# Nine instead of six feed-forward pairs as seven block products in the first layer, with other PSUM banks for the down products

## The chip, the cores and the metric

The kernel runs on one core of one Trainium2 chip. The metric is the device time of one execution in microseconds (us). A core has a matrix engine (TensorE, PE in the profile), a vector engine (VectorE, DVE), a scalar engine (ScalarE, ACT), GpSimd (POOL) and a sync engine (SyncE, SP) that only issues transfers. Matrix products go to PSUM, eight banks of 512 float32 columns on 128 partitions, and are copied out of it by ACT or DVE. Each engine works through its own queue in order. An instruction that waits holds up all that stands behind it on the same engine.

## The reference

Two layers of a decoder trunk over 528 tokens (16 learned ones and 512 real ones) of width 1024. Each layer is a mixer (attention, a convolution module, a short convolution, an output projection) and a feed-forward part (FFN). The change touches the FFN:

```python
def ffn_sublayer(h, pre_g, post_g, w_up, conv_w, w_down):
    u = rms_norm(h, pre_g)
    z = jnp.einsum("bld,df->blf", u, w_up)          # 1024 -> 2 x 2816
    z = causal_depthwise_conv(z, conv_w)            # 3 taps
    g, up = jnp.split(z, 2, axis=-1)
    y = jnp.einsum("blf,fd->bld", jax.nn.silu(g) * up, w_down)   # 2816 -> 1024
    return h + rms_norm(y, post_g)
```

All data are float32.

## The kernel before, in words

Activations lie transposed: 128 channels on the partitions, the 528 tokens along the free dimension. Every float32 operand is split in two float32r numbers, high and low, and a product is made of three matmuls (high x high, low x high, high x low). A weight block of 128 output columns is loaded as one tile `raw` (512 KB) by SP, ACT casts it to `whi`, DVE subtracts to get `wlo`. `next_w` (and `prefetch`, `prep_one` beneath it) keeps three blocks ready; `whi` and `wlo` have three buffers, so a cast waits until TensorE has finished the block three before. `raw_tile` gives out three `raw` buffers and, within the FFN, four more in the tile `h`, which lies in DRAM (`h_dram`) meanwhile.

**The FFN.** The 2816 hidden channels are 22 pairs f = 0 to 21, a gate block and an up block of 128 columns each. They come in three parts of 8, 7 and 7 pairs (`PARTS`): f = 0 to 7, 8 to 14, 15 to 21. After each part come the eight down products m = 0 to 7 of that part. The result of a down product is copied (part 0, ACT, L2403) or added (part 1, DVE, L2405) to `yp`.

**An ordinary pair** takes for each of two blocks 8 row groups x 3 matmuls x 2 token halves, 96 matmuls of 264 columns in the first layer, into the bank pairs 6-7 and 2-3.

**A pair as seven products** (`seven_pair`, L2285) splits the 1024 rows in two halves and the tokens in two halves, and forms the 2 x 2 blocks with seven block products instead of eight, of 12 matmuls each: 84 matmuls of 264 columns (258 in the second layer). It uses three banks, 0 to 2 and 3 to 5 in turn. It needs sums of token blocks (`ts`, made once in each layer by `normalised`), and sums of weight blocks, which lie in DRAM as `w_sum`. Of the up block it then loads three parts in place of one: "c" and "b" of 512 KB from `w_sum` and "d" of 256 KB from the weights. "c" is split to `whi`, `wlo`; "b" to `shi`, `slo`, of which there is one buffer; "d" to the spare tile `y7`. The order of use in a pair is: gate block, c, b, gate, c, b, d. The first layer has six such pairs (15 to 20), the second twelve (8 to 13 and 15 to 20): `SEVEN`.

**Where the weight sums are made.** (1) In the mixer, by a planner that places all of the mixer's work by costs (`sum_steps` through `flow.op`, lowest priority): copies DRAM to DRAM by SP, then three accumulating DMAs by POOL (L533). (2) In the FFN by `tick` (L2196): at each pair one of the four steps of a sum, behind a small POOL copy that waits for the newest gate result. (3) During the down products of parts 0 and 1, two each, by `down_sums`: loads by POOL into `h`, four DVE additions, stores by POOL (L602). In the first layer, the sums of 15 and 16 come from its own mixer, and its `tick` makes those of f = 8 and 9 of the second layer at f = 1 to 8.

**Splits made ahead.** Six blocks of the second layer's input projection are split during part 1 of the first layer and stored in DRAM as `w_split`: `store_one` (L657) is called once at each pair f = 8 to 14. Each call splits the block fetched by the call before (ACT L662 to `shi`, DVE L663 to `slo`), stores both by POOL (L666), and fetches the next block by SP (L671).

**Order.** In the FFN the order of each engine's instructions comes from a list scheduler, which works on program order and modelled times; the engines hold to it at run time. `tc.issue_after(x)` fixes that what is traced in it stands behind x on x's own engine; it is an order, not a wait for another engine. In the mixer and in the last down products the planner sets the order.

The four lines that choose the banks and the place of the splits (before):

```python
tiles = [mmt((6, 2)[m % 2]) if seven else mmt() for m in some]   # L2386
if l == 0 and part == 1:                                          # L2342
    store_one()
todo = deque(step for to, place in ((l, 2), (l + 1, 0)) ...)      # L2194
```

Of the kernel before, what the change touches and what calls it, by code (L numbers as in the profile page):

```python
# [10 lines left out]
F32 = mybir.dt.float32  # L11
# [11 lines left out]
DEPTH = 2  # L23
# [5 lines left out]
PARTS = (8, 7, 7)  # L29


SEVEN = ((15, 16, 17, 18, 19, 20), (8, 9, 10, 11, 12, 13, 15, 16, 17, 18, 19, 20))
SUMS = {0: (0, 2, 0), 1: (2, 4, 2)}
DOWN_SUMS = 2
SUM_US, SUM_LAT, SUM_EVERY = 0.9, 9.0, 40.0
K2 = KD // 2
SB = K2 * P
# [336 lines left out]
def stt_us(n):  # L374
    return 0.22 + 0.00102 * n
# [13 lines left out]
def tile_hybrid_trunk(ctx: ExitStack, tc: tile.TileContext, xT, wflat, pv_d, out):  # L389
    nc = tc.nc  # L390
# [156 lines left out]

    def sums_at(l, place):

        counts = SUMS.get(l, ())  # L550
        n0 = sum(counts[:place])
        return SEVEN[l][n0:n0 + counts[place]] if place < len(counts) else ()

    pw_place = [None]

# [5 lines left out]
            return pw_place[0][:, :n] if tag == "whi" else pw_place[0][:, n:2 * n]  # L561
        return T(wx[0], [P, WCHUNK], F32R, tag) if i in wide else T(wp, [P, CHUNK], F32R, tag)

    parts, last_load, last_low = deque(), [None], [None]
    spare, n_raw = [None], [0]

    def spare_tile(j):
# [39 lines left out]

    def down_sums(l, part):

        fs = SEVEN[l][-2 * DOWN_SUMS:][DOWN_SUMS * part:DOWN_SUMS * (part + 1)]  # L610
        at = {}
        for j, f in enumerate(fs):
            load, add, store = down_sum(l, f, j % 2)
            for m, op in ((2 * j - 1, load), (2 * j + 1, add), (2 * j + 1 + (j < 2), store)):
                at.setdefault(m, []).append(op)
        return at

    def prep_one():
        i = wpos[0]
        if i >= len(chunks):  # L620
            return
        if i in seven_up:
            if not parts:
                t = sums[seven_up[i]]
                parts.extend((("c", t[:, 1::2]), ("b", t[:, 0:3:2]), ("d", flat_w(i)[:, SB:])))
            kind, src = parts.popleft()
            wpos[0] += not parts
            raw = raw_tile()
            sz = SB if kind == "d" else 2 * SB
            nc.sync.dma_start(raw[:, :sz] if kind == "d" else raw[:, :sz].rearrange("p (e s) -> p e s", e=2),  # L630
                              src)
            if kind == "b":
                hi, lo = (T(tx[0], [P, 2 * SB], F32R, t) for t in ("shi", "slo"))
            elif kind == "c":
                hi, lo = (T(wp, [P, CHUNK], F32R, t) for t in ("whi", "wlo"))
            else:
                hi, lo = y_pair(max(PARTS) - 1)
            nc.scalar.copy(hi[:, :sz], raw[:, :sz])
            last_low[0] = nc.vector.tensor_sub(lo[:, :sz], raw[:, :sz], hi[:, :sz].bitcast(F32))
            ready.append((i, tuple(t[:, :sz].rearrange("p (k n) -> p k n", n=P) for t in (hi, lo))))  # L640
            return
        wpos[0] += 1
        kn, n = chunks[i][3], chunk_cols(chunks[i])
        sz = kn * n
        raw = raw_tile()
        last_load[0] = nc.sync.dma_start(raw[:, :sz], wflat[offs[i]:offs[i] + P * sz].rearrange("(p s) -> p s", p=P))
        hi, lo = wtile(i, "whi"), wtile(i, "wlo")
        nc.scalar.copy(hi[:, :sz], raw[:, :sz])  # L648
        last_low[0] = nc.vector.tensor_sub(lo[:, :sz], raw[:, :sz], hi[:, :sz].bitcast(F32))  # L649
        ready.append((i, tuple(t[:, :sz].rearrange("p (k n) -> p k n", n=n) for t in (hi, lo))))  # L650
# [1374 lines left out]
    with tc.tile_pool(name="pre", bufs=2, reuse_waits="tile") as sp, tc.manual_schedule(engines=every):  # L2025
# [64 lines left out]
    for l in range(DEPTH):  # L2090
# [23 lines left out]
        with tc.tile_pool(name=f"fp{l}", bufs=2, reuse_waits="tile") as fp:  # L2114
# [76 lines left out]
            h7 = [(i0, i0 + n7), (L - n7, L)]  # L2191
            late_ups = deque()
            seven = SEVEN[l]
            todo = deque(step for to, place in ((l, 2), (l + 1, 0)) for f in sums_at(to, place) for step in sum_steps(to, f))  # L2194

            def tick(src):  # L2196

                if todo:
                    t = nc.gpsimd.tensor_copy(ticks, src.bitcast(F32))
                    with tc.issue_after(t.ins):  # L2200
                        todo.popleft()()
# [62 lines left out]
            building = [None]  # L2264
# [71 lines left out]
            g = {}  # L2336
            f0 = 0
            for part, nf in enumerate(PARTS):
                for f in range(f0, f0 + nf):
                    if g:  # L2340
                        tick(g[max(g)][0][:, :1])
                    if l == 0 and part == 1:  # L2342
                        store_one()
                    if f in seven:
                        seven_pair(f)
                        if f == seven[-1]:
                            spare[0] = None
                            with tc.issue_after(last_load[0].ins):
                                for k in range(0, KD, 2):
                                    nc.sync.dma_start(h[:, k:k + 2], h_dram[:, k:k + 2])  # L2350
                        continue
                    finish_pair()
                    if seven and f == 2:
                        building[0] = normalised()
                    for i in (2 * f, 2 * f + 1):
                        if i < len(zs):
                            continue
                        if i < FIRST["w_out"]:
                            scaled(i, [first.ps[hf, i] for hf in range(2)])
                            continue  # L2360
                        w = next_w()
                        ps = mmt((6, 2)[i % 2]) if ts else mmt()
                        mm3({hf: ps[:, hf, :iws[hf]] for hf in range(2)}, w, range(KD), u_in)
                        if ts:
                            for (a, z), hf in zip(i_spans, range(2)):
                                nc.scalar.copy(zs[i % len(zs)][:, off + a - i0:off + z - i0], ps[:, hf, :z - a])
                            continue
                        scaled(i, [ps[:, :, :H]] if i0 == 0 else [ps[:, hf, :iws[hf]] for hf in range(2)])
                    g[f] = ffn_gate(f)
                    if building[0] is not None and f < PARTS[0] - 1:  # L2370
                        with tc.issue_after(mul_ins[0].ins):
                            build(5)
# [7 lines left out]
                if part < len(PARTS) - 1:  # L2380
# [2 lines left out]
                        op()  # L2383
                    for some in ((0, 1), *((m,) for m in range(2, KD))):
                        ws = [next_w() for _ in some]
                        tiles = [mmt((6, 2)[m % 2]) if seven else mmt() for m in some]  # L2386
                        for group in (ks[:-1], ks[-1:]):
                            for w, ps in zip(ws, tiles):
                                where = {"start": group[0] == ks[0], "stop": group[-1] == ks[-1]}
                                if final:  # L2390
                                    mm3({0: ps[:, 0, :2 * fw]}, w, group, lambda b, k, hf, f0=f0: g[f0 + k][b][:, :2 * fw], **where)
                                else:
                                    mm3({hf: ps[:, hf, :fw] for hf in range(2)}, w, group, grhs, **where)
                        if building[0] is not None:
                            with tc.issue_after(glo_ins[0].ins):
                                build(99)
                        for m, ps in zip(some, tiles):
                            if final:
                                d, src = yp[:, m, t0:], ps[:, 0, :2 * fw]
                            else:  # L2400
                                d, src = two(yp[:, m, t0:]), ps[:, :, :fw]
                            if part == 0:
                                evac = glo_ins[0] = nc.scalar.copy(d, src)  # L2403
                            else:
                                evac = nc.vector.tensor_add(d, d, src)  # L2405
                            for op in more.pop(m, ()):
                                with tc.issue_after(evac.ins), tc.issue_after(last_low[0].ins):
                                    op()
                else:
                    assert not todo and building[0] is None  # L2410
# [6 lines left out]
                    if not final:  # L2417
                        raw = list(zip(*[g[f0 + k] for k in range(nf)], y_pair(nf)))
# [65 lines left out]
```

## Time and profile before

| | us |
|---|---|
| median of three runs | 1269.38 (1269.15 to 1270.08) |
| the profiled execution | 1270.68 |
| its span, first to last instruction | 1269.0 |
| PE busy | 1249.8 |
| DVE busy | 920.9 |
| ACT busy | 705.2 |
| POOL busy | 162.0 |

In the trace, the first layer's FFN takes its first down products from about 353.5 us, its part 1 pairs run from 401.0 to 483.1, the down products of part 1 to 524.2, and part 2 follows. The second layer's seven-product pairs of part 1 begin at 1030.5. A line of the profile names the line of the kernel, the engine, the operation, and output<-inputs. `h<-in_w_dram` is a weight load into the lent tile. The bracket in a timeline line gives the idle time of the engine just before, and what ended it.

### The profile page before, as it was taken

To read this page: it belongs to the slowest core of one execution; us is meant where nothing else is said; L and a number is where in the kernel's file an instruction comes from. 1 tells how busy PE (TensorE), PEld (TensorE's weight loads), DVE (VectorE), ACT (ScalarE), POOL (GpSimd) and SP (SyncE) were. 2 spreads that over 40 slices of the span, in tenths; PEclk is the share of its full clock that TensorE was granted. 3 is DMA by queue.
4 is the path that set the end of the run, shared out by engine and by line. 5 is a ranking of instruction groups with operands and counts; after the bars stand their busy time and mean duration, and the time that the engine had idled before them with its cause. 6 is when DMAs were issued, how large, how long until landed. Compare 5 with 4: busy or idle time off the path is not lost.

```text
span 1269.0 us, 24272 instructions
## 1 busy us (share of the span) xinstructions
PE 1249.8 (98%) x9590; PEld 1198.2 (94%) x9590; DVE 920.9 (73%) x1569; ACT 705.2 (56%) x1365; POOL 162.0 (13%) x343
## 2 busy tenths in 40 slices
PE   8999999999999999999999999999999999999997
PEld 8998898999999999999999988999999799979996
DVE  7887866589874665587688878656799748756954
ACT  7254576654444643476673545775554447526763
POOL 1324311001101100000003244110021000000000
PEclk9999999999999999999999999999999999999999
DMA  7257231726558634544552584547166655475611
GB/s 243 81 155 175 72 102 53 249 86 151 182 164 313 212 112 142 205 165 144 192 205 61 159 191 113 143 118 233 70 166 184 172 176 169 152 241 160 202 61 67
DMA packets 76146, 197.93 MB, mean 156 GB/s; under 512 B 8240, under 2 KB 18608, under 8 KB 75520
## 3 DMA queue, kind: packets, MB, share of 16 engines
q1 hardware_dynamic: 64048, 162.69, 40.0%
q0 software_dynamic: 11984, 33.69, 11.1%
q8 instruction: 75, 1.23, 0.4%
q14 instruction: 39, 0.32, 0.1%
HBM read 162.17 MB, written 44.30 MB: 163 GB/s over the span
## 4 chain that ended last, share of the span: by engine, by line
PE 66%; DVE 2%; ACT 1%; issue 0%; DMA 0%; POOL 0%; DVEq 0%; ACTq 0%
PE psum L833 45%; PE psum L2281 14%; PE psum L1403 2%; PE psum L1667 2%; PE psum L970 1%; PE psum L1633 1%; PE psum L1589 0%; DMA h<-w_sum 0%; DVE yp L1046 0%; PE psum L1733 0%; PE psum L1319 0%; DVE h L1056 0%; POOL dm L1604 0%; DVE ulo L1064 0%; DVE wlo L649 0%
## 5 line engine op out<-in xcount | busy, mean ns | idle before, releaser
L833 PE MATMUL psum<-y,whi 128*128 128x264 f32 (+3 forms) x1968 | 384.7, 299 | 2.7 <-ACT yp L2403 1.4
L833 PEld LDWEIGHTS psum<-y,whi 128*128 128x128 f32 x1968 | 305.1, 188 | 17.2 <-ACT yp L2403 2.6
L833 PE MATMUL psum<-uhi,whi 128*128 128x264 f32 (+1 forms) x1264 | 310.3, 288 | 1.6 <-ACT uhi L2065 0.8
L833 PE MATMUL psum<-ulo,whi 128*128 128x264 f32 (+1 forms) x1264 | 304.1, 284 | 0.6 <-DVE ulo L2067 0.4
L833 PE MATMUL psum<-uhi,wlo 128*128 128x264 f32 (+1 forms) x1264 | 303.2, 284 | 0.0
L833 PE MATMUL psum<-y,wlo 128*128 128x264 f32 (+3 forms) x984 | 273.9, 297 | 1.1 <-DVE wlo L789 1.1
L833 PEld LDWEIGHTS psum<-uhi,whi 128*128 128x128 f32 x1264 | 216.0, 188 | 5.9 <-issue 1.6
L833 PEld LDWEIGHTS psum<-ulo,whi 128*128 128x128 f32 x1264 | 216.1, 188 | 1.3 <-DVE ulo L2067 0.6
L833 PEld LDWEIGHTS psum<-uhi,wlo 128*128 128x128 f32 x1264 | 215.6, 188 | 0.0
L833 PEld LDWEIGHTS psum<-y,wlo 128*128 128x128 f32 x984 | 177.6, 188 | 6.7 <-DVE wlo L789 1.6
L2169 DVE SCALAR_TENSOR_TENSOR c<-zs,pv,c 128x528 f32<-128x528 f32 (+1 forms) x176 | 130.9, 757 | 18.4 <-ACT c L2167 16.4
L648 ACT CAST whi<-raw 128x1024 fp32r<-128x1024 f32 (+1 forms) x67 | 68.2, 1021 | 98.4 <-PE psum L833 72.6
L789 DVE TENSOR_TENSOR wlo<-raw,whi 128x1024 fp32r<-128x1024 f32 (+2 forms) x80 | 95.4, 1203 | 29.8 <-ACT whi L785 29.5
L649 DVE TENSOR_TENSOR wlo<-raw,whi 128x1024 fp32r<-128x1024 f32 (+1 forms) x67 | 79.4, 1185 | 28.1 <-ACT whi L648 28.0
L785 ACT CAST whi<-raw 128x1024 fp32r<-128x1024 f32 (+2 forms) x80 | 81.7, 1031 | 24.9 <-PE psum L833 18.0
L1149 DVE SCALAR_TENSOR_TENSOR cacc<-apad,pv,cacc 128x528 f32<-128x528 f32 x120 | 87.7, 772 | 0.1
L2167 ACT ACTIVATE c<-zs,pv 128x528 f32<-128x528 f32 (+1 forms) x88 | 63.1, 727 | 7.0 <-DVE zs L2132 2.7
L2281 PE MATMUL psum<-uhi,whi 128*128 128x258 f32 (+1 forms) x216 | 61.2, 284 | 0.0
L2281 PE MATMUL psum<-ulo,whi 128*128 128x258 f32 (+1 forms) x216 | 61.0, 283 | 0.0
L2281 PE MATMUL psum<-uhi,wlo 128*128 128x258 f32 (+1 forms) x216 | 60.5, 282 | 0.0
L2281 PE MATMUL psum<-t,shi 128*128 128x258 f32 (+1 forms) x288 | 54.2, 283 | 0.0
L1667 PE MATMUL psum<-pf,vals 128*128 128x400 f32 (+3 forms) x160 | 50.7, 399 | 0.6 <-POOL pf L1647 0.6
(273 smaller groups left out, 2193.2 us busy)
## 6 DMA issues: line engine op xcount, KB each, us to landing
raw<-in_w_dram SPq DMA_DIRECT2D x115, 512.0 KB, 4.5
h<-in_w_dram SPq DMA_DIRECT2D x27, 512.0 KB, 4.8
raw<-in_w_dram SPq DMA_DIRECT2D x30, 448.0 KB, 5.1
raw<-w_sum SPq DMA_DIRECT2D x18, 512.0 KB, 5.1
h<-w_sum SPq DMA_DIRECT2D x18, 512.0 KB, 5.4
h<-in_w_dram POOLq DMA_DIRECT2D x16, 512.0 KB, 3.8
w_sum<-h POOLq DMA_DIRECT2D x16, 512.0 KB, 5.3
w_sum<-in_w_dram SPq DMA_DIRECT2D x20, 256.0 KB, 5.0
```

Of the source, the lines that this page charges most:

```text
L648: nc.scalar.copy(hi[:, :sz], raw[:, :sz])
L649: last_low[0] = nc.vector.tensor_sub(lo[:, :sz], raw[:, :sz], hi[:, :sz].bitcast(F32))
L785: nc.scalar.copy(box["hi"][:, :sz], box["raw"][:, :sz])
L789: nc.vector.tensor_sub(lo[:, :sz], box["raw"][:, :sz], box["hi"][:, :sz].bitcast(F32))
L833: nc.tensor.matmul(d, lhsT=w[a][:, k, cols], rhs=rhs(b, k, hf), start=start and i == 0 and p == 0, stop=stop and i == n - 1 and p == 2)
L970: nc.tensor.matmul(ps, lhsT=om_d, rhs=box["c"][:, i, :], start=j + i == 0, stop=j + 1 == n_parts and i == tiles[-1])
L1149: nc.vector.scalar_tensor_tensor(conv[j], in0=src, in1=conv[j], scalar=col("a_dw_w", CK * j + i), op0=ALU.mult, op1=ALU.add)
L1403: nc.tensor.matmul(ps[:n, :nw], lhsT=(uhi, ulo)[ui][:, k, P * b:P * b + n], rhs=w[wi][:, k % 4, :], start=k == 0 and p == 0, stop=k == KD ...
L1667: nc.tensor.matmul(acc[:, s0 - qa:qz - qa], lhsT=vals[:, b].rearrange("p h d -> p (h d)")[:, o:o + P], rhs=box["p"], start=b == 0, stop=b ...
L2167: nc.scalar.activation(dst, src[:, 2:2 + 2 * fw], AF.Copy, scale=wtap(2, t))
L2169: nc.vector.scalar_tensor_tensor(dst, in0=src[:, i:i + 2 * fw], scalar=wtap(i, t), in1=dst, op0=ALU.mult, op1=ALU.add)
L2281: nc.tensor.matmul(psum[:, bank, :n7], lhsT=w[a][:, k0 + k, :], rhs=rhs(b, k), start=start and k == 0 and p == 0, stop=stop and k == K2 - ...
```

## The change

`SEVEN` of the first layer grows from six pairs to nine: f = 11, 12 and 13 are added. The table `SUMS` now names the pairs for each place: in the first layer, 11 to 13 in the mixer (three sums where two were), 15 and 16 by `tick` at f = 1 to 8, 17 to 20 in the down products as before. The second layer's 8 and 9 move to the ticks from f = 14 on (`NEXT_SUMS`). The second layer's own table is as it was. `store_one` is called at f = 8, 8, 9, 9, 10, 10, 11 instead of once at each of 8 to 14. In both layers the down products of parts 0 and 1 use three bank pairs, 4-5, 6-7 and 2-3, in turn. In both layers, the load, the cast and the subtraction of a block b stand behind those of the block prepared just before it among b, c and d, which is its c.

```diff
-SEVEN = ((15, 16, 17, 18, 19, 20), (8, 9, 10, 11, 12, 13, 15, 16, 17, 18, 19, 20))
-SUMS = {0: (0, 2, 0), 1: (2, 4, 2)}
-DOWN_SUMS = 2
+SUMS = (((), (11, 12, 13), (15, 16), (17, 18), (19, 20)),
+        ((8, 9), (10, 11, 12, 13), (15, 16), (17, 18), (19, 20)))
+SEVEN = tuple(sorted(sum(places, ())) for places in SUMS)
+NEXT_SUMS, AHEAD_SPLITS = 13, (8, 8, 9, 9, 10, 10, 11)
...
     def sums_at(l, place):
-        counts = SUMS.get(l, ())
-        n0 = sum(counts[:place])
-        return SEVEN[l][n0:n0 + counts[place]] if place < len(counts) else ()
+        return SUMS[l][place] if l < DEPTH else ()
...
     def down_sums(l, part):
-        fs = SEVEN[l][-2 * DOWN_SUMS:][DOWN_SUMS * part:DOWN_SUMS * (part + 1)]
-        for j, f in enumerate(fs):
+        for j, f in enumerate(sums_at(l, 3 + part)):
...
-            nc.sync.dma_start(raw[:, :sz] if kind == "d" else raw[:, :sz].rearrange("p (e s) -> p e s", e=2),
-                              src)
+            with ExitStack() as order:
+                for x in last if kind == "b" else ():
+                    order.enter_context(tc.issue_after(x.ins))
+                load = nc.sync.dma_start(raw[:, :sz] if kind == "d" else raw[:, :sz].rearrange("p (e s) -> p e s", e=2), src)
...
-            nc.scalar.copy(hi[:, :sz], raw[:, :sz])
-            last_low[0] = nc.vector.tensor_sub(lo[:, :sz], raw[:, :sz], hi[:, :sz].bitcast(F32))
+            with ExitStack() as order:
+                for x in last if kind == "b" else ():
+                    order.enter_context(tc.issue_after(x.ins))
+                high = nc.scalar.copy(hi[:, :sz], raw[:, :sz])
+                last_low[0] = nc.vector.tensor_sub(lo[:, :sz], raw[:, :sz], hi[:, :sz].bitcast(F32))
+            last[:] = load, high, last_low[0]
...
-            todo = deque(step for to, place in ((l, 2), (l + 1, 0)) for f in sums_at(to, place) for step in sum_steps(to, f))
+            todo, later = (deque(step for f in sums_at(to, place) for step in sum_steps(to, f)) for to, place in ((l, 2), (l + 1, 0)))
             def tick(src):
+                if max(g) + 1 >= NEXT_SUMS:
+                    todo.extend(later)
+                    later.clear()
...
-                    if l == 0 and part == 1:
+                    for _ in range(AHEAD_SPLITS.count(f) if l == 0 else 0):
                         store_one()
...
-                        tiles = [mmt((6, 2)[m % 2]) if seven else mmt() for m in some]
+                        tiles = [mmt((4, 6, 2)[m % 3]) if seven else mmt() for m in some]
```

More of the change, by code (lines that the diff above doesn't have):

```diff
@@ L562, in wtile @@
         return T(wx[0], [P, WCHUNK], F32R, tag) if i in wide else T(wp, [P, CHUNK], F32R, tag)
-    parts, last_load, last_low = deque(), [None], [None]
+    parts, last_load, last_low, last = deque(), [None], [None], []
     spare, n_raw = [None], [0]
@@ L2409, in tile_hybrid_trunk @@
                 else:
-                    assert not todo and building[0] is None
+                    assert not todo and not later and building[0] is None
                     if seven:
```

## The prediction

> **What bounds the kernel now.** I read the page first, then who waited for whom on TensorE, then the busy time by stretches, then the timeline at each place where TensorE stood.
>
> ```profile
> span 1269.0 us, 24272 instructions
> PE 1249.8 (98%) x9590; PEld 1198.2 (94%) x9590; DVE 920.9 (73%) x1569; ACT 705.2 (56%) x1365; POOL 162.0 (13%) x343
> PEclk9999999999999999999999999999999999999999
> PE 66%; DVE 2%; ACT 1%; issue 0%; DMA 0%; POOL 0%; DVEq 0%; ACTq 0%
> PE psum L833 <- ACT yp L2403: 1.4, 2, 1.0
> PE psum L833 <- DVE yp L2405: 0.3, 1, 0.3
> ```
>
> TensorE is busy for 1249.8 of 1269.0 us, with a granted clock of nine tenths or more in every slice. The other engines matter only where they make it stand. So the change is worth the matmuls that it removes, plus the stalls that it removes, less those that it brings. Two of its waits name the copies of down products (L2403, L2405).
>
> **Seven instead of eight block products.** Three pairs lose 12 of 96 matmuls each, 36 together. Matmul rows overlap, so their own length (about 284 ns) is no price. The stretch that holds exactly the seven ordinary pairs of part 1 gives the interval:
>
> ```profile
> 401.00:483.10 82.10, 82.10 (x675) 82.10 (x674) 49.33 (x56) 43.90 (x72) 6.40 (x12) 1.00 0.50 167
> 1030.50:1090.00 59.50, 59.50 (x496) 59.34 (x495) 46.34 (x61) 43.44 (x78) 1.42 (x3) 1.00 0.53 167
> ```
>
> 82.10 us over 7 x 96 = 672 matmuls (the 675 count neighbours cut by the edges) are 0.122 us each, so a pair takes 11.7 us and 36 matmuls are **4.4 us**. The second row is the same arrangement as the new one, the second layer's pairs 8 to 13: TensorE is busy for 59.50 of 59.50 us with DVE at 46.3 and ACT at 43.4, so a run of seven-product pairs in part 1 does not wait for the copies, the extra casts (c, b, d for one up block) or the loads. I take the 4.4 us whole. The primer matmuls (one for each of banks 1 and 4) are two before and after.
>
> [...]
>
> **Three bank pairs for the down products.** With two, product m = 2 needs the banks of m = 0, whose last matmuls come just before those of m = 1. All five stalls of these stages:
>
> ```profile
> 365.12 0.41 PE L2304 MATMUL psum<-uhi,ones_r 128*128 128x264 f32 x2
> 365.99 0.75 PE L833 MATMUL psum<-y,whi 128*128 128x264 f32 x4 [0.46 <-ACT yp L2403]
> 366.57 0.28 PE L833 MATMUL psum<-y,wlo 128*128 128x264 f32 x1
> ...
> 493.00 0.40 PE L833 MATMUL psum<-y,wlo 128*128 128x264 f32 x2
> 493.48 0.76 PE L833 MATMUL psum<-y,whi 128*128 128x264 f32 x4
> ...
> 994.57 0.39 PE L833 MATMUL psum<-y,whi 128*128 128x512 f32 x1
> 994.80 0.40 PE L833 MATMUL psum<-y,wlo 128*128 128x512 f32 x1
> 996.17 0.73 PE L833 MATMUL psum<-y,whi 128*128 128x512 f32 x2 [0.97 <-ACT yp L2403]
> ...
> 1012.80 0.40 PE L833 MATMUL psum<-y,wlo 128*128 128x512 f32 x1
> 1013.27 0.73 PE L833 MATMUL psum<-y,whi 128*128 128x512 f32 x2
> ...
> 1111.91 0.40 PE L833 MATMUL psum<-y,wlo 128*128 128x512 f32 x1
> 1112.62 0.73 PE L833 MATMUL psum<-y,whi 128*128 128x512 f32 x2 [0.31 <-DVE yp L2405]
> ```
>
> The bracket is only the idle time; the loss is the next start less the start that was due, 0.12 us after a 264-column matmul and 0.23 after a 512-column one (994.57 to 994.80). First: the second primer starts at 365.24, the next was due at 365.36 and came at 365.99, 0.63 lost. Likewise 493.48 - 493.24 = 0.24, 996.17 - 995.03 = 1.14, 1013.27 - 1013.03 = 0.24, 1112.62 - 1112.14 = 0.48: 2.73 together. Four matmuls after the first stall took 0.58 instead of 0.49 us, a slow restart of 0.1 that I count at each of the five. **3.2 us** go: with three pairs, the copy of m has two products (more than 5 us) to finish. What is late next is the weight block, whose cast waits for the third block before; it is not later than now.
>
> **A new wait at the end of part 0.** m = 7 takes banks 6-7 (7 mod 3 = 1), and the next pair of the first layer, f = 8, still ordinary, starts in 6-7 at once. Before, m = 7 lay in 2-3.
>
> ```profile
> 400.96 1.05 ACT L648 CAST whi<-raw 128x1024 fp32r<-128x1024 f32 x1 [4.27 <-PE psum L833]
> 401.91 0.60 ACT L2403 COPY yp<-psum 128x528 f32<-128x528 f32 x1
> 401.00 0.41 PE L833 MATMUL psum<-uhi,whi 128*128 128x264 f32 x2
> ```
>
> TensorE goes on at 401.00; the copy of m = 7 ends at 402.51, behind a cast. In that order the wait is 1.6 us with the restart. It is nothing if the scheduler lets the second block of f = 8 (banks 2-3, free) go first, as it let the primers of a later pair into the first stall above. Between 0 and 1.6, I take **0.9 lost**, a copy without the cast ahead. The other changes of stage use banks that are free: the second layer's f = 8 begins in 0 to 2; f = 15 in 3 to 5 in the first layer, where m = 6 ended a product earlier.
>
> **Block b behind c.** In the second layer b is now cast 14 us before c:
>
> ```profile
> 1010.22 1.05 ACT L638 CAST shi<-h 128x1024 fp32r<-128x1024 f32 x1 [5.33 <-DMA h<-w_sum]
> 1012.64 0.58 ACT L2403 COPY yp<-psum 128x512 f32<-128x512 f32 x1
> 1024.52 1.05 ACT L638 CAST whi<-raw 128x1024 fp32r<-128x1024 f32 x1 [4.05 <-PE psum L833]
> ```
>
> ACT stood for 5.33 us on b's load with a down product's copy behind it (the stall at 1012.80, counted already). Behind c this goes. At f = 11, c's cast can begin when the first block of f = 10 is used, at 401.0 + 2.5 x 11.73 = 430.3; two casts (1.05 each) and one subtraction of 1.2 make b ready by 433.7. It is used after 24 matmuls of f = 11: 401.0 + 3 x 11.73 + 2.9 = 439.1. Nothing lost; with 5 us of slack.
>
> **The splits, two to a pair.** They share `shi`, `slo` with b, one buffer each. So b of f = 11 comes after all six.
>
> ```profile
> L662 ACT CAST shi<-h x4: 1047/1048/1049, 378.9 to 425.6; 128x1024 fp32r<-128x1024 f32 x4
> L662 ACT CAST shi<-raw x2: 1049/1050/1050, 403.2 to 436.9; 128x1024 fp32r<-128x1024 f32 x2
> L663 DVE TENSOR_TENSOR slo<-h,shi x4: 1226/1226/1226, 380.0 to 426.7; 128x1024 fp32r<-128x1024 f32 x4
> L666 POOL DMA_DIRECT2D w_split<-slo x6: 533/533/536, 381.5 to 439.5; - x6
> w_split<-slo POOLq DMA_DIRECT2D x6, 512.0 KB, 6.7
> 374.70:391.90 17.20, 17.20 (x144) 17.20 (x143) 11.03 (x13) 7.36 (x10) 2.12 (x4) 1.00 0.95 349
> ```
>
> One round is the subtraction at 380.0, the store at 381.5 and its landing 6.7 us later: 8.2 us until `slo` can be written again. Now there is a round every 11.6 us (378.9 to 436.9 in five). Packed, six rounds end at 380.0 + 6 x 8.2 = 429.2, and b could be subtracted by 430.4: before the 433.7 above, so no loss. The casts and subtractions number the same, and DVE has 32.8 us free in the 82.1 of part 1 (49.3 busy). Queued behind a split that waits for its buffer are, on ACT, casts and PSUM copies, on DVE the convolution; TensorE waits for those only after about a block (5.9 us).
>
> **The sums.** The mixer's third sum adds three POOL DMAs. The second layer's mixer has four sums already; the same matmul in both layers:
>
> ```profile
> 115.19 0.28 PE L1613 MATMUL psum<-dm,ones_r 128*128 128x264 f32 x1
> 186.60 0.68 PE L1319 MATMUL psum<-apad,bd 128*128 128x264 f32 x2 [0.38 <-ACT q L1615]
> 746.70 0.31 PE L1613 MATMUL psum<-dm,ones_r 128*128 128x264 f32 x1
> 818.11 0.68 PE L1319 MATMUL psum<-apad,bd 128*128 128x264 f32 x2 [0.39 <-ACT q L1615]
> 774.78 1.19 POOL L533 DMA_DIRECT2D w_sum<-in_w_dram  x1
> ```
>
> 71.41 us lie between the marks in both, though in the second layer a third sum (from 774.78) falls between them. So it costs nothing; a POOL wait in a bad place would be about 1 us, the 1.19 us of one issue. The ticks at f = 1 to 8 do eight steps as before, for other pairs. The eight steps moved to f = 14 to 21 put six copies into SP's queue and six DMAs into POOL's. Behind POOL's stand only the down sums' loads and stores, wanted much later; SP's copies wait for nothing, and its transfers have room (share 0.50 over part 1). Nothing.
>
> **Sum.** 4.4 + 3.2 - 0.9 = 6.7 us. The profiled execution took 1270.68, 1.3 more than the median of 1269.38; it would become 1264.0, and the median **1262.7**. Its own range is 1261.5 to 1264.5, from the 0 to 1.6 of the new wait and half a microsecond of order in the mixer.
>
> **Rivals.**
>
> *The bank change gives nothing* (another wait takes the stalls' place, as the cast that shares ACT with the copies). Then 4.4 - 0.9 = 3.5 us are gained: 1265.9. For it: at 400.96 a cast stands ahead of a copy. Against: weights were there whenever TensorE went on. Chance 0.13.
>
> *A few microseconds of new stalls* at f = 8 to 11, where a late split blocks ACT or DVE by about one landing beyond its slack (6.7 us less 2 to 3): 1266.8 to 1270, no measurable change. For it, from the list of waits:
>
> ```profile
> ACT shi L662 <- DMA h<-in_w_dram: 9.9, 4, 4.0
> ```
>
> Already, ACT stands 9.9 us in four waits for split loads, up to 4.0 in one. Against: none of them made TensorE stand, and half of the work moves to the down products, where ACT is idle for 9.84 of 17.20 us. Chance 0.12.
>
> *b of f = 11 comes late, and the kernel is slower.* If fetches still run one to a pair (the lent tiles are handed out in turn with the weights'), the last split stays at 436.9 at best, its `slo` is stored at 439.5 and lands at 446.2, and b is subtracted by 447.5: 8.2 us after its need at 439.3 (439.1 and the net 0.2 us of shift until there): 1270.9. If the denser traffic adds an estimated 1 us to each of the five rounds, b is ready at 452.5, 13.2 late: 1275.9. It makes the kernel measurably slower once b is ready later than about 448.5 (439.3 + 6.7 + 2.5). For it: DMA is at 0.95 of its time, 349 GB/s, in the stretch from 374.7 where the packed splits would begin. Against: TensorE was busy for all 17.20 us of that stretch, and the work does run ahead of its place now: the split called at f = 9 (412.7) is cast at 378.9, and with two calls to a pair the later ones come earlier in program order. Chance 0.12.
>
> [...]
>
> **How the numbers follow.** The forecast has 0.63. About 0.2%, 2.5 us, is what a measurement of this kernel can tell from no change. Faster by more: forecast and first rival, 0.76. Within: the second, 0.12. Slower: the third, 0.12. The range goes from 1260.8, the sum without the new wait and with 1 us of luck, to 1270.5, which takes in the first two rivals; the third lies beyond it.
>
> **What would show it.** Right: 36 matmuls fewer; part 1's pairs of the first layer shorter by 4.4 us; no wait of TensorE for L2403 or L2405 at m = 2; L638 casts of `whi` ahead of `shi` at f = 8 and 11; six L662 casts before about 425; TensorE without a gap between 425 and 445. A gap near 401 on ACT's copy of m = 7 shows the new wait. Wrong: a gap near 439 released by `slo` (third rival), by `zs` copies between 400 and 440 (second), or marks in the first mixer further apart than 71.4 us.

## The result, and the profile after

The change takes the median from 1269.93 (1269.15 to 1271.13, six runs) to 1262.86 us (1262.10 to 1264.00, six runs): 7.1 us, a ratio of 0.9942, 95% interval 0.9932 to 0.9952. The profiled executions took 1270.68 and 1262.10; 1.5 us of their difference of 8.6 is that one lies above its median and the other below.

The page of the changed kernel, span, engines and the chain of waits by engine:

```profile
span 1260.4 us, 24292 instructions
PE 1244.2 (99%) x9554; PEld 1194.4 (95%) x9554; DVE 926.0 (73%) x1581; ACT 710.3 (56%) x1377; POOL 175.9 (14%) x360
PE 94%; DVE 2%; ACT 1%; DMA 1%; POOL 1%; issue 0%; SPq 0%; DVEq 0%; ACTq 0%
```

36 matmuls fewer. Neither L2410 nor L2412 (L2403 and L2405 before, the copy and the addition of a down product) is among TensorE's waits any more. From 352 to 478 us there is one wait, and it is new:

```profile
PE psum L2288 <- ACT zs L2373: 0.4, 1, 0.4
```

Busy time by stretches: down products of part 0, pairs of part 1, and the second layer's pairs of part 1.

```profile
352.60:399.10 46.50, 46.50 (x385) 46.50 (x385) 29.36 (x35) 21.65 (x28) 6.11 (x11) 1.00 0.71 254
399.20:477.30 78.10, 77.75 (x640) 77.53 (x639) 54.52 (x67) 47.90 (x81) 6.12 (x13) 1.00 0.65 218
1022.80:1094.80 72.00, 72.00 (x602) 72.00 (x601) 54.88 (x74) 49.18 (x88) 2.12 (x4) 1.00 0.54 171
```

TensorE never stops in the first and third. In the second it stands for 0.35 us. The timeline of the start of part 1 (TensorE, then ACT):

```profile
398.92 0.41 PE L837 MATMUL psum<-y,wlo 128*128 128x264 f32 x2
399.17 0.41 PE L837 MATMUL psum<-uhi,whi 128*128 128x264 f32 x2
...
399.12 1.05 ACT L652 CAST whi<-h 128x1024 fp32r<-128x1024 f32 x1 [0.71 <-PE psum L837]
400.08 0.59 ACT L2410 COPY yp<-psum 128x528 f32<-128x528 f32 x1
```

The copy of m = 7 is late, as feared (behind a cast, until 400.67), but TensorE goes on at 399.17 without a bracket. So its first matmuls of f = 8 cannot be those into banks 6-7: the scheduler put the second block (banks 2-3) first. The one gap of part 1, with ACT's lines ahead of its end:

```profile
435.85 0.28 PE L2288 MATMUL psum<-uhi,wlo 128*128 128x264 f32 x1
436.49 0.51 PE L2288 MATMUL psum<-t,whi 128*128 128x264 f32 x2 [0.35 <-ACT zs L2373]
...
434.47 1.05 ACT L652 CAST whi<-h 128x1024 fp32r<-128x1024 f32 x1 [0.59 <-PE psum L837]
435.52 0.65 ACT L2183 ACTIVATE c<-c 128x528 f32<-128x528 f32 x1
436.07 0.64 ACT L2373 COPY zs<-psum 128x264 f32<-128x264 f32 x2
```

f = 11 wants its third bank, bank 2, after 24 matmuls. The second block of the ordinary pair f = 10 lay in 2-3, and its copy stands on ACT behind a cast and an activation. 0.52 us are lost (436.49 less the 435.97 that was due).

The splits, and blocks c and b of f = 11 behind them:

```profile
L666 ACT CAST shi<-h x3: 1048/1049/1052, 378.3 to 418.2; 128x1024 fp32r<-128x1024 f32 x3
L670 POOL DMA_DIRECT2D w_split<-slo x6: 531/532/533, 380.9 to 423.5; - x6
...
430.56 1.05 ACT L641 CAST whi<-raw 128x1024 fp32r<-128x1024 f32 x1
431.51 1.05 ACT L641 CAST shi<-h 128x1024 fp32r<-128x1024 f32 x1
...
432.78 1.22 DVE L642 TENSOR_TENSOR slo<-h,shi 128x1024 fp32r<-128x1024 f32 x1
```

The sixth split is stored from 423.5, c is cast before b, and b is ready at 434.0 (432.78 + 1.22).

### The profile page after: what moved, and what is told of

It is laid out like the page before. It is cut to its first block, busy times and chain, and to the rows that moved or that the text cites. A ratio compares the mean times of both kernels' runs of the same rounds, so it can differ in the third digit from the quotient of the medians.

```text
span 1260.4 us, 24292 instructions
## 1 busy us (share of the span) xinstructions
PE 1244.2 (99%) x9554; PEld 1194.4 (95%) x9554; DVE 926.0 (73%) x1581; ACT 710.3 (56%) x1377; POOL 175.9 (14%) x360
## 4 chain that ended last, share of the span: by engine, by line
PE 94%; DVE 2%; ACT 1%; DMA 1%; POOL 1%; issue 0%; SPq 0%; DVEq 0%; ACTq 0%
PE psum L837 63%; PE psum L2288 17%; PE psum L1407 5%; PE psum L1671 3%; PE psum L1637 2%; PE psum L974 1%; PE psum L1593 1%; PE psum L1737 1%; PE psum L1323 1%; DMA raw<-in_w_dram 0%; POOL dm L1608 0%; DMA h<-in_x_dram 0%; DVE yp L1050 0%; DVE h L1060 0%; PE psum L1617 0%
## 5 line engine op out<-in xcount | busy, mean ns | idle before, releaser
L837 PE MATMUL psum<-uhi,whi 128*128 128x264 f32 (+1 forms) x1168 | 292.2, 289 | 1.5 <-ACT uhi L2069 0.8
L837 PE MATMUL psum<-ulo,whi 128*128 128x264 f32 (+1 forms) x1168 | 286.0, 284 | 0.6 <-DVE ulo L2071 0.4
L837 PE MATMUL psum<-uhi,wlo 128*128 128x264 f32 (+1 forms) x1168 | 285.3, 284 | 0.0
L837 PEld LDWEIGHTS psum<-uhi,whi 128*128 128x128 f32 x1168 | 201.7, 189 | 5.9 <-issue 1.6
L837 PEld LDWEIGHTS psum<-ulo,whi 128*128 128x128 f32 x1168 | 201.8, 189 | 1.3 <-DVE ulo L2071 0.6
L837 PEld LDWEIGHTS psum<-uhi,wlo 128*128 128x128 f32 x1168 | 201.5, 189 | 0.0
L2288 PE MATMUL psum<-uhi,whi 128*128 128x258 f32 (+1 forms) x252 | 71.4, 284 | 0.0
L2288 PE MATMUL psum<-ulo,whi 128*128 128x258 f32 (+1 forms) x252 | 71.3, 283 | 0.0
L2288 PE MATMUL psum<-uhi,wlo 128*128 128x258 f32 (+1 forms) x252 | 70.8, 283 | 0.0
L2206 POOL COPY cols<-y 128x1 f32<-128x1 f32 x24 | 18.4, 767 | 334.7 <-ACT y L2187 334.4
```

Of the source, the lines that this page charges most:

```text
L837: nc.tensor.matmul(d, lhsT=w[a][:, k, cols], rhs=rhs(b, k, hf), start=start and i == 0 and p == 0, stop=stop and i == n - 1 and p == 2)
L2288: nc.tensor.matmul(psum[:, bank, :n7], lhsT=w[a][:, k0 + k, :], rhs=rhs(b, k), start=start and k == 0 and p == 0, stop=stop and k == K2 - ...
```

## The experiments

Twelve kernels. Those of one group were timed beside the kernel before, whose medians were 1270.22 (first four), 1270.14 (next three), 1270.07 (next four) and 1270.08 (the last).

| kernel | median (lowest to highest) | ratio to before, 95% |
|---|---|---|
| E1 change, two bank pairs | 1269.62 (1266.35 to 1272.96) | 0.9991 [0.9981, 1.0001] |
| E2 before, three bank pairs | 1270.92 (1267.77 to 1273.16) | 1.0002 [0.9993, 1.0011] |
| E3 change, six pairs | 1267.14 (1266.08 to 1268.09) | 0.9975 [0.9964, 0.9985] |
| E4 change, b not behind c | 1267.89 (1265.42 to 1272.25) | 0.9989 [0.9977, 1.0000] |
| E5 change, one split to a pair | 1277.35 (1276.01 to 1279.25) | 1.0061 [1.0048, 1.0075] |
| E6 change, ten pairs | 1266.59 (1263.56 to 1268.39) | 0.9971 [0.9962, 0.9980] |
| E7 change, free bank for f = 10 | 1262.11 (1261.57 to 1262.65) | 0.9940 [0.9927, 0.9952] |
| E8 before, b behind c | 1269.86 (1269.04 to 1270.09) | 0.9995 [0.9986, 1.0004] |
| E9 before, three bank pairs, b behind c | 1267.14 (1266.05 to 1269.85) | 0.9980 [0.9970, 0.9990] |
| E10 E1 with the free bank | 1267.12 (1265.97 to 1267.83) | 0.9975 [0.9965, 0.9985] |
| E11 E4 with the free bank | 1266.25 (1263.79 to 1271.65) | 0.9973 [0.9960, 0.9986] |
| E12 ten pairs, free bank, five splits | 1267.30 (1265.42 to 1268.07) | 0.9976 [0.9965, 0.9987] |

The same stages in the profiled executions, in us from the first matmul of a stage to the first of the next, read off TensorE's timeline (L1, L2: first and second layer):

| stage | before | E8 | E2 | E9 | after | E7 | E1 | E10 | E4 | E11 |
|---|---|---|---|---|---|---|---|---|---|---|
| L1 downs, part 0 | 47.55 | 47.55 | 46.61 | 46.61 | 46.61 | 46.61 | 47.55 | 47.56 | 46.61 | 46.61 |
| L1 pairs, part 1 | 82.07 | 82.07 | 82.13 | 82.13 | 78.20 | 77.79 | 82.23 | 79.52 | 83.57 | 80.38 |
| L1 downs, part 1 | 41.08 | 41.06 | 40.73 | 40.73 | 40.76 | 40.81 | 41.32 | 41.32 | 40.77 | 40.77 |
| L2 part 0 with downs | 119.57 | 119.25 | 117.44 | 117.44 | 117.39 | 117.35 | 119.24 | 118.98 | 117.37 | 117.34 |
| L2 pairs, part 1 | 72.01 | 71.99 | 74.59 | 72.12 | 72.12 | 72.12 | 72.05 | 72.02 | 73.77 | 73.87 |
| L2 downs, part 1 | 39.64 | 39.65 | 39.07 | 39.07 | 39.07 | 39.07 | 39.63 | 39.62 | 39.07 | 39.07 |
| L2 part 2 | 72.12 | 72.04 | 76.16 | 72.20 | 72.04 | 72.04 | 72.04 | 72.04 | 72.63 | 73.98 |

The theory to be tested was the prediction's: 36 matmuls and five stalls, the order of b and c worth nothing, packed splits just in time. The rivals: the banks or the order are worth more or less than that.

**E1. Two bank pairs again, on the changed kernel.**

```diff
-tiles = [mmt((4, 6, 2)[m % 3]) if seven else mmt() for m in some]
+tiles = [mmt((6, 2)[m % 2]) if seven else mmt() for m in some]
```

> The changed kernel with the two bank pairs 6-7 and 2-3 for the down products again. My theory (TensorE is the bound, and its stalls for the copies of m = 0 are the price of two pairs): the five stalls come back, 2.7 us of lost starts and 0.5 us of restarts, so 3.2 us more than the changed kernel, about 1266.1 and a ratio of 0.997 to the kernel before. Rival (the stalls went for another reason, such as the order of block b): as the changed kernel, 1262.9, with no TensorE wait on L2410.

6.8 us lost instead of 3.2. The four down stages account for 3.9 of it in the profile (0.94, 0.56, 1.85, 0.56), near the forecast. The other 4.0 lie in part 1 of the first layer, which has no down products. Timeline of TensorE and ACT, and one of ACT's waits from 375 to 440 us:

```profile
438.12 0.28 PE L2288 MATMUL psum<-uhi,wlo 128*128 128x264 f32 x1
440.85 0.51 PE L2288 MATMUL psum<-t,whi 128*128 128x264 f32 x2 [2.45 <-ACT zs L2373]
...
438.95 0.64 ACT L2183 ACTIVATE c<-c 128x528 f32<-128x528 f32 x1 [1.64 <-DVE c L2173]
...
440.43 0.65 ACT L2373 COPY zs<-psum 128x264 f32<-128x264 f32 x2
...
ACT shi L666 <- DMA w_split<-shi: 12.6, 4, 5.1
```

It is the gap of f = 11 again, with 2.6 us lost instead of 0.5. The 24 matmuls behind it take 4.6 us instead of 2.9, another 1.6. ACT's split casts now stand 12.6 us for earlier stores to land, against 4.4 in the changed kernel (there the casts at 397.37, 402.50 and 418.20 each begin within 0.1 us of the landing of such a store, though the profile names something else for the first two). The copy of f = 10 comes late in ACT's queue.

**E2. Three bank pairs on the kernel before.** The same line, the other way.

> The kernel before with only the three bank pairs. My theory: the five stalls go without any other part of the change, and at the end of part 0 the second block of f = 8 fills the wait for m = 7; 3.2 us less, about 1266.7, ratio 0.9975. In the second layer ACT may still stand about 5 us on block b's load, but with a product more of slack TensorE doesn't wait for it. Rival (the bank change needs block b behind c): one or two of the second layer's stalls stay, 0.3 to 1.5 us less gained.

No gain instead of the 3.2 us expected, although all four down stages are as short as after the change. It is given back in the second layer's parts 1 and 2 (74.59 and 76.16). The waits, then ACT and TensorE at the start of part 2:

```profile
PE psum L2281 <- ACT whi L648: 3.4, 2, 2.3
...
1131.87 1.05 ACT L638 CAST shi<-h 128x1024 fp32r<-128x1024 f32 x1 [6.39 <-DMA h<-w_sum]
1143.47 1.04 ACT L648 CAST whi<-h 128x1024 fp32r<-128x1024 f32 x1 [6.21 <-DMA h<-in_w_dram]
...
1144.57 0.39 PE L2281 MATMUL psum<-uhi,whi 128*128 128x258 f32 x1 [2.31 <-ACT whi L648]
```

b's cast of `shi` goes ahead of c's and stands 6.39 us for its load. Behind it ACT stands 6.21 us for the next pair's gate weights, and TensorE waits for their cast. The gap, and slow matmuls behind it that cost another 1.6 us, are nearly all of the 4.1 us that part 2 loses. The kernel before has the same cast at almost the same time:

```profile
1143.72 1.05 ACT L648 CAST whi<-h 128x1024 fp32r<-128x1024 f32 x1 [5.58 <-DMA h<-in_w_dram]
```

But its part 2 begins at 1142.02 and that of E2 at 1139.24. TensorE came to this part 2.8 us sooner and its weights only 0.25 us.

**E3. Six pairs, on the changed kernel.**

```diff
-SUMS = (((), (11, 12, 13), (15, 16), (17, 18), (19, 20)),
+SUMS = (((), (), (15, 16), (17, 18), (19, 20)),
```

> The changed kernel with f = 11 to 13 as ordinary pairs again and no sums in the first mixer; all else kept. My theory: 36 matmuls of 0.122 us come back, 4.4 us, and the wait of 0.5 us at the start of f = 11 goes: 3.9 us more than the changed kernel, 1266.8, ratio 0.9975. Rival (the mixer's sums cost TensorE about 1 us for each wait of POOL): 2 us more or less, 1264.9, with a shorter first mixer.

1267.14, near the 1266.8 expected: the three pairs are worth 4.3 us (1267.14 less 1262.86).

**E4. b free to go ahead of c, on the changed kernel.**

```diff
-                for x in last if kind == "b" else ():
+                for x in ():
```

(twice: for the load, and for the cast and the subtraction)

> The changed kernel without the order of block b behind c. The scheduler puts b's cast ahead of c's again at f = 11 (four casts and copies earlier) and at f = 15 of the first layer. My theory: with three bank pairs there is slack for a copy that stands behind b's load, so TensorE does not wait: 0 to 0.6 us more than the changed kernel. Rival (the order is what makes the rest work): b at f = 11 waits on ACT for the last split's store, and the copies behind it stop TensorE for 2 us or more.

5.0 us lost: the expectation of little or nothing falls. Timeline and stretches of 4 us at f = 11:

```profile
435.91 0.28 PE L2288 MATMUL psum<-uhi,wlo 128*128 128x264 f32 x1
439.16 0.81 PE L2288 MATMUL psum<-t,whi 128*128 128x264 f32 x2 [2.97 <-ACT zs L2373]
439.77 0.42 PE L2288 MATMUL psum<-t,wlo 128*128 128x264 f32 x1
439.99 0.64 PE L2288 MATMUL psum<-t,whi 128*128 128x264 f32 x2
...
432.00:436.00 4.00, 4.00 (x35) 3.98 (x33) 3.97 (x6) 1.27 (x2) 0.00 (x0) 1.00 0.41 132
436.00:440.00 4.00, 1.03 (x6) 0.84 (x5) 2.32 (x3) 2.74 (x6) 0.00 (x0) 0.79 0.42 137
440.00:444.00 4.00, 4.00 (x20) 4.00 (x20) 2.34 (x4) 0.70 (x2) 0.00 (x0) 0.50 0.21 70
444.00:448.00 4.00, 4.00 (x30) 4.00 (x30) 1.00 (x2) 2.24 (x4) 0.00 (x0) 0.86 0.00 0
```

The gap of f = 11 is 2.97 us, and behind it TensorE is "busy" for 4.00 of 4.00 us with 20 matmuls instead of 35, at a granted clock of 0.50. The gap costs 3.1 us. The 27 matmuls from 439.16 to 445.21 take 6.0 us instead of 3.3, 2.7 more. Less the 0.5 that the changed kernel loses here too, these are the 5.4 us that part 1 is longer than after the change. As the rival has it, b's cast now stands for the last split's store: it begins at 425.65, within 0.1 us of the landing, after 1.80 us of waiting. How that makes the copy of f = 10 late, some ten instructions further on in ACT's queue, is not shown. The second layer's parts 1 and 2 lose another 1.7 and 0.6 us; this execution lies 1.8 us above its median.

**E5. One split to a pair, on the changed kernel.**

```diff
-NEXT_SUMS, AHEAD_SPLITS = 13, (8, 8, 9, 9, 10, 10, 11)
+NEXT_SUMS, AHEAD_SPLITS = 13, (8, 9, 10, 11, 12, 13, 14)
```

> The changed kernel with the splits ahead called once at each of f = 8 to 14 again. My theory (one buffer of shi and slo serves splits and blocks b in turn, a round of 8.2 us): splits then stand between the blocks b of f = 11, 12 and 13. After b of f = 11 is used (8.8 us into the pair) a split takes 2.3 us and 6.7 us to land, then b of f = 12 takes 2.3 us: ready about 20 us after the start of f = 11, needed at 10.3 + 2.9 = 13.2. So about 7 us of TensorE's idle time at each of f = 12 and 13: 10 to 17 us more than the changed kernel, about 1277, slower than the kernel before. Rival (the place of the splits does not matter, as they are off TensorE's path): 1262.9.

14.5 us lost against the change, 7.2 against before. The time is the one expected, but by luck: the first loss is in another place. From 399 to 500 us TensorE waits longest at the start of f = 9, for ACT's copy of a block of f = 8, and ACT for the load of a block d.

```profile
PE psum L837 <- ACT zs L2373: 3.3, 1, 3.3
...
412.69 0.62 ACT L641 CAST y<-raw 128x512 fp32r<-128x512 f32 x1 [10.99 <-DMA raw<-in_w_dram]
413.21 1.04 ACT L652 CAST whi<-h 128x1024 fp32r<-128x1024 f32 x1
414.15 0.65 ACT L2373 COPY zs<-psum 128x264 f32<-128x264 f32 x2
```

A cast stands 10.99 us for its load, with weights and copies behind it. Shorter gaps of TensorE follow at 459.20, 468.40 and 501.54 (1.20, 1.90 and 2.40 us).

**E6. Ten pairs** (f = 10 too), with the splits called three to a pair.

```diff
-SUMS = (((), (11, 12, 13), (15, 16), (17, 18), (19, 20)),
+SUMS = (((), (10, 11, 12, 13), (15, 16), (17, 18), (19, 20)),
-NEXT_SUMS, AHEAD_SPLITS = 13, (8, 8, 9, 9, 10, 10, 11)
+NEXT_SUMS, AHEAD_SPLITS = 13, (8, 8, 8, 9, 9, 9, 10)
```

> The changed kernel with f = 10 added as a tenth pair of seven products (its sum made in the mixer with the other three), and the splits called at f = 8, 8, 8, 9, 9, 9, 10. My theory (the rounds of 8.2 us bound the splits): the sixth split lands at about 430.6 as now, b of f = 10 can be ready at 431.9, and is needed at 422.6 + 2.9 = 425.5: 6.4 us of idle TensorE, less 1.5 us for 12 matmuls: 4.9 us more than the changed kernel, about 1267.8. Rival (the rounds go faster when called earlier): 1.5 us less, 1261.4.

3.7 us slower than the change in spite of 12 matmuls fewer (4.9 expected). The sixth split is cast at 418.85, no earlier than after the change (418.20), and b's cast begins at 426.41, within 0.1 us of the landing of that split's store, after 2.17 us of waiting: so far the theory. But what TensorE waits for is a copy behind b's cast, not b. The gap has moved one pair ahead with the first seven-product pair, and the slow restart with it:

```profile
424.71 0.28 PE L2288 MATMUL psum<-uhi,wlo 128*128 128x264 f32 x1
428.73 0.51 PE L2288 MATMUL psum<-t,whi 128*128 128x264 f32 x2 [3.74 <-ACT zs L2373]
...
429.00:433.00 4.00, 4.00 (x23) 4.00 (x23) 2.30 (x3) 1.81 (x4) 0.00 (x0) 0.59 0.65 243
```

**E7. The second block of f = 10 in banks 4-5**, which f = 11 does not use.

```diff
-                        ps = mmt((6, 2)[i % 2]) if ts else mmt()
+                        ps = mmt((6, 4 if l == 0 and f == 10 else 2)[i % 2]) if ts else mmt()
```

> The changed kernel with the second block of f = 10 in banks 4-5 instead of 2-3, so that the third bank of f = 11 (bank 2) is free. My theory: the wait of TensorE for the zs copy at the start of f = 11 goes, 0.5 us less than the changed kernel, 1262.4, too little for the time alone but to be seen in the trace. Rival: the wait moves to the next bank or to block c, 1262.9.

The gap is gone and part 1 takes 77.79 instead of 78.20 us. In the medians the 0.75 us between the two can't be told from nothing: the intervals of the ratios overlap.

**E8. Only b behind c, on the kernel before** (the lines with `last` of the change's diff).

> The kernel before with only the order of block b behind c (two bank pairs, six pairs, splits as before). Theory A (the two parts pay only together): the down products' stalls stay, since their cause, the copies of the banks two products back, is untouched; only the 0.24 us at 1013.27, where a copy stood behind b's cast that waited for its load, can go. 0 to 0.4 us less than the kernel before: about 1269.9. Rival B (the order alone is worth the 3.2 us, and the banks nothing): 1267.0, with the stalls at 366 and 996 still in the trace but shorter.

Alone the order does nothing that can be measured. In the profile, the second layer's part 0 with its downs is 0.3 us shorter.

**E9. E8 with three bank pairs** (the line of E2).

> The kernel before with three bank pairs and with b behind c, without the three more pairs. Theory A (the banks alone gained nothing because b, cast ahead of c, held ACT when the next part's first weights were due, 2.5 to 4.7 us in the second layer): both together give the 3.2 us of the five stalls, and no wait at 1028, 1030 or 1142: 1266.9. Rival B (the waits in the second layer come from the earlier down products themselves, whatever the order of b and c): 1270 to 1271, with TensorE still waiting for ACT whi casts at 1028 and 1142.

As theory A has it: 1267.14, and no wait in the second layer's parts. At the same place as in E2, gate weights are now cast 3.3 us earlier, 1.83 us behind the first matmul of part 2 (1138.34) instead of 4.23:

```profile
1140.17 1.05 ACT L654 CAST whi<-h 128x1024 fp32r<-128x1024 f32 x1 [3.07 <-DMA h<-in_w_dram]
```

Banks alone gain nothing, order alone nothing, both together 2.9 us, interval 1.3 to 3.8.

**E10. E1 with the free bank of E7** (both lines above).

> The changed kernel with two bank pairs for the down products, as in the first experiment, and with the second block of pair f = 10 in a bank pair that f = 11 does not use. Theory A (two bank pairs cost the 3.2 us of the five stalls, and the rest of the 6.8 us seen was the wait of f = 11 for the copy of f = 10, 2.6 us, and the slow matmuls behind that gap): with that wait gone the loss is 2.9 to 3.4 us against the same kernel with three bank pairs (1262.1): 1265.0 to 1265.5, and no matmuls at half pace near 440. Rival B (the two banks cost more by themselves): 1266.5 or more.

5.0 us lost against E7: theory A falls, and the time is rival B's. The down stages cost 3.6 (0.95, 0.51, 1.63, 0.55), as it says, and nothing runs at half pace (granted clock 1.00 from 440 to 448 us, 36 matmuls in the second half of that), but part 1 still loses 1.7. With bank 2 free, the next thing in ACT's late queue is waited for:

```profile
439.60 0.28 PE L2288 MATMUL psum<-t,wlo 128*128 128x264 f32 x1
440.70 0.39 PE L2288 MATMUL psum<-uhi,whi 128*128 128x264 f32 x1 [0.81 <-ACT whi L652]
...
ACT shi L666 <- DMA w_split<-shi: 11.5, 4, 3.5
```

**E11. E4 with the free bank of E7.**

> The changed kernel with block b free to go ahead of c, as in the fourth experiment, and with the second block of f = 10 in a free bank pair. Theory A (of the 5.0 us lost there, 3.1 were the wait for the copy of f = 10 and the half pace behind it was a consequence of that gap; only the 1.9 us of waits at 1030 to 1144 belong to the order itself): 1264.0, the matmuls after 436 at full pace. Rival B (the wait moves on: b's cast ahead of c still holds ACT, so that c or b itself is late at f = 11): a gap of 2 to 3 us stays near 436 to 442, followed by half pace, and 1266.5 to 1268.

4.1 us lost against E7, between the two theories. Nothing runs at half pace (granted clock 1.00 from 438 to 450 and from 1139 to 1147 us). The waits are three smaller ones in part 1 (2.6 us more than E7) and, as in E2 and E4, the second layer's weights (1.8 and 1.9 us more in parts 1 and 2; this execution lies 2.2 us above its median). Of the three waits in this line one is in part 1 of the first layer, at 440; the others end at 1029 and 1143:

```profile
PE psum L2288 <- ACT whi L652: 2.9, 3, 1.6
```

So the order is worth its 4 us mainly for itself, not only through the bank of f = 10.

**E12. Ten pairs, the free bank moved to f = 9, five splits ahead instead of six.**

```diff
-NEXT_SUMS, AHEAD_SPLITS = 13, (8, 8, 9, 9, 10, 10, 11)
+NEXT_SUMS, AHEAD_SPLITS = 13, (8, 8, 8, 9, 9, 9)
-MASK = "111111000000000000000000"
+MASK = "111110000000000000000000"
-                        ps = mmt((6, 2)[i % 2]) if ts else mmt()
+                        ps = mmt((6, 4 if l == 0 and f == 9 else 2)[i % 2]) if ts else mmt()
```

(with the `SUMS` of E6; `MASK` marks the blocks that are split ahead)

> A candidate better than the changed kernel: ten pairs as seven block products (f = 10 added), the second block of f = 9 in a bank pair that f = 10 does not use, and only five blocks split ahead (two each at... three at f = 8 and three calls at f = 9), so that the split tiles come free one round of about 8 us earlier; the sixth block is cast and subtracted in the second layer instead. Theory A (with ten pairs it was only the late split tiles and the bank of f = 9's copy that cost 3.9 us and its slow restart): five splits are stored by about 420, block b of f = 10 is ready by about 422 and wanted at 399.2 + 2 x 11.73 + 2.9 = 425.6, so 12 matmuls of 0.122 us are gained, 1.5 us against the changed kernel with the free bank (1262.1): 1260.6, if the sixth block's cast and subtraction (1.05 and 1.23 us) find idle time in the second layer. Rival B (part 1 has no slack for a tenth pair: some other copy or cast on ACT is then late at f = 10 or 11): a gap of 1 us or more between 420 and 445 and 1262 to 1266. Rival C (the sixth block's work in the second layer stands in the way): no gap there, but part 0 of the second layer or the mixer's end longer by 1 to 2 us, about 1262.5.

Slower than the change by 4.4 us. Theory A falls. Rivals B and C each hold in part, though B's gap lies outside its 420 to 445 us and the time above both. TensorE waits twice in part 1, at 413.72 and 429.59,

```profile
PE psum L837 <- ACT whi L652: 1.1, 1, 1.1
PE psum L2288 <- DVE wlo L653: 0.6, 1, 0.6
```

and the stretch from the last down products of the first layer to the second layer's FFN, 592.68 to 908.70, is 1.7 us longer than after the change (591.01 to 905.35). Nearly all of that is one wait for DVE's `zs` in the mixer, 2.34 us at 661.38 where the change has 0.70; that the sixth block's work causes it is not shown. No version here is measurably faster than the change.

## Why the prediction was right, and where it was not

The total was forecast at 1262.7 and came at 1262.86. Step by step:

- **36 matmuls, 4.4 us: right.** Part 1 without any stall takes 82.13 us with ordinary pairs (E9) and 77.79 with three seven-product pairs (E7), 4.3 less.
- **Five stalls, 3.2 us: gone, but wrong in what they depend on.** The four down stages are 0.9, 0.3, 2.2 and 0.6 us shorter in the profiled executions, 4.0 together and 0.8 more than the term. In the medians the two edits give 2.9 (E9). The step that failed is the sentence on block b behind c, "Nothing lost", with its gain put down as "counted already". E2 shows that without it the 3.2 us are given back, as waits for the cast of gate weights at the starts of the second layer's parts; E8 and E9 show that the two edits pay only together. What was missed: that step asked only where ACT's wait for b's load hurt in the kernel before. It hurt little there, because TensorE came later to the next part. At the start of the second layer's part 2 this can be read off: the cast of the next gate weights begins 1.70 us after the part's first matmul before, 4.23 in E2 and 1.83 in E9; it takes 1.05 us, and TensorE in E2 wants the block 3.0 us after that matmul. For the other places it is argued from E2. That "what is late next is the weight block; it is not later than now" holds only with the order fixed.
- **The new wait at the end of part 0, 0.9 us: did not come.** The lower bound held. ACT's copy was as late as in the row of before, but TensorE had the block for the other bank pair ahead of it.
- **An unforeseen wait, 0.5 us.** "The other changes of stage use banks that are free" overlooked the one inside part 1, from the last ordinary pair to the first seven-product pair, where bank 2 passes from f = 10 to f = 11. E7 shows that it is this bank.
- **The splits: right.** The last was stored at 423.5 + 0.5 and b was ready at 434.0, against forecasts of 429.2 for the landing (it landed at 430.6) and 433.7. E3 and E9 differ in the packed splits and in where weight sums are made, and have the same median, so the two together cost nothing that shows. The third rival's wait for `slo` at f = 11 came in no run; in E5 the late loads struck ACT's queue first, at f = 9. The second rival's mechanism, a late split that holds ACT and the copies behind it, did not come with the change either, but E6 shows it, and E4 in part.
- **The mixer's third sum: nearly right.** The first layer's mixer is 0.5 us shorter at one POOL wait (behind 115.19 before, behind 114.84 after), and 70.86 instead of 71.41 us lie between the prediction's marks; the second layer's, with the last down products ahead of it, is 0.6 us longer (591.01 to 905.35 against 597.05 to 910.80). Both are below what the medians can tell.

So the total was right partly by luck. Two small errors, 0.9 us too much and 0.5 us too little, stood against each other. The gain was 7.1 us instead of 6.7, from a median of 1269.93 instead of the 1269.38 that the forecast began with. The forecast's own range, 1261.5 to 1264.5, does not follow from its two terms, which give 1261.3 to 1263.9.

What stays open: why ACT's split casts stand so much longer for their stores in E1 and E10 (12.6 and 11.5 us) than after the change (4.4). The order of ACT's casts and copies from part 0's down products on differs between E1 and the change, since the scheduler arranges it anew for every edit; the runs do not separate this from the banks themselves.

## What to carry to other kernels

When a change removes a stall, ask what that stall gave time to: here the loads and casts of the next part, so that the edit paid nothing until a second edit, worthless alone, put them in the right order. Where work passes from one way of using PSUM to another, list for every bank who held it last and where that holder's copy stands in its engine's queue. And allow for more than its length when you price a gap on TensorE: of eight gaps of 1.90 to 3.74 us here six were followed by slow matmuls, at a granted clock of 0.50 to 0.74 over 4 us.

## What the hardware showed

A gap on TensorE can be followed by slow matmuls. After gaps of 1.90 and 3.33 (E5), 2.31 (E2), 2.45 (E1), 2.97 (E4) and 3.74 us (E6) the granted clock in a stretch of 4 us behind them falls to 0.71, 0.57, 0.66, 0.74, 0.50 and 0.59, in this order. In E4 (439.77 to 439.99) and E6 (430.74 to 430.96) matmuls then start 0.22 us apart instead of 0.12. Summed over these stretches and their neighbours, 4 us times what is missing to a clock of 1.00, the loss is 1.7 us after five of the gaps and 3.4 in E4. By TensorE's timeline the slow matmuls cost 1.6 us more than the gap itself in E1, E2 and E6, and 2.7 in E4.

Length alone does not decide it here. After the gaps of 0.35 (the change), 0.81 (E10) and 1.64 us (E11) the clock stays at 1.00, but no fall shows after 2.40 us in E5 (to 501.54) and 2.34 us in E12 (to 661.38) either. The mean granted clock of these two executions is 0.997 and 1.000; with one more loss of 1.7 us in spans of 1275.6 and 1264.0 us it would be 0.996 and 0.999, by an estimate from these figures. What tells the two gaps from the six is not shown; no run moved a gap on purpose.

The clock also shows in the spread of E1 (6.6 us, the change 1.9): its executions with a mean granted clock of 0.999 or more took 1266.35 to 1268.68 us, those with 0.998 or less 1269.22 to 1272.96.
